# Sigmoid off the last stored gates, gelu at eviction, gates fetched two blocks ahead, combination in another queue

## The chip, the cores and the metric

The kernel runs on one core of one Trainium2 chip. The metric is the device time of one execution in microseconds. A core has a matrix engine (PE, with its weight loads shown as PEld), a vector engine (DVE), a scalar engine for activations (ACT), GpSimd (POOL), and SP, which in this kernel issues nearly all DMAs. Each engine works through its own instructions in the order in which they stand, and waits on semaphores for the others.

## The reference

One layer of a decoder trunk over 1024 prompt positions and 32 sample positions (1056 columns in all), width 1024, all in fp32:

```
h = layer_norm(ALPHA * x + 0.5 * swiglu(x, f1_w1, f1_w3, f1_w2), ln1_g, ln1_b)
z = h @ w_in + b_in                       # q, k, v | u, v of the SGU | gates ga, gb
...
att = combine_groups(outs, lses)          # 3 dilated window groups, softmax weights of the denominators
yb = u * (tril(W_s) LN(v) + b)            # u, v = gelu(uv), chunks of 128
mix = (sigmoid(ga) * (att @ w_oa) + sigmoid(gb) * (yb @ w_ob)) @ w_out
h = layer_norm(ALPHA * h + mix, ln2_g, ln2_b)
h = layer_norm(ALPHA * h + 0.5 * swiglu(h, f2_w1, f2_w3, f2_w2), ln3_g, ln3_b)
```

The prompt's attention has three groups (window, dilation) = (128, 1), (512, 4), (2048, 16) with four heads each. The sample rows attend to stored keys and values.

## The kernel before

Activations lie transposed: 128 channels on the partitions, positions on the free axis, cut into four chunks of 264 columns. A product in fp32 is made of three passes on rounded halves (`mm3`: high x high, high x low, low x high), so one 128 x 264 block over a depth of 1024 is 24 matmuls of 264 columns (`dense8`), and one over a depth of 512 or 256 is 12 or 6. Most large products use a Strassen-like scheme of seven products (`pair`, `hidden`, `seven`).

The program runs `ffn`, `widen`, `mix`, `ffn`. `widen` makes z, 42 blocks of 128 channels by 1056 columns, and stores each in DRAM (`zD`). Blocks 0 to 17 are q, k, v; 18 to 21 are u and 22 to 25 v of the SGU; 26 to 33 and 34 to 41 are the gates ga and gb. Ten of the sixteen gates are made by plain products (`gate8`): the first `NLEAD` = 6 (34 to 39) at the head of `widen`, while the layer norm of the chunks is finishing, and the last `NTAIL` = 4 (30 to 33) in `mix`, where their matmuls fill PE beside the attention. Of the six in `widen`, the first `CHUNKED` come chunk by chunk, all of a chunk's as soon as that chunk is normed; their weights are loaded during the end of `ffn` into tiles of the slot pool. The others come unit by unit. All other blocks come from `pair`, two blocks at a time, which gathers the seven products on ACT and DVE and sends the results to `zD`.

`mix` has two products per output block n of eight: `local(n)` makes gb x (yb @ w_ob), where `mt[n]` is first the gate 34 + n loaded from `zD` and is multiplied by the product at eviction (L1491); the main loop then loads the gate 26 + n into `ta`, multiplies it by att @ w_oa, adds the two (L1552) and splits the sum into halves for `w_out`. `local` of the first four blocks runs ahead of `split_att`, that of the last four inside the loop.

Side work is written as generators in three queues, and `tick` moves them: `bg` (the attention of one head group, `attend`, and `sample_rows`), `slow` (one step per tick: the sample attention, the combination of groups, the joining of the samples) and `mid` (three steps per tick: the SGU). `combine(hp)` is appended when the third group of a half is finished. It fetches the minima and sums of the three groups in twelve small loads from `mlD`, makes the coefficients on DVE, writes them to `cD`, and fetches them back broadcast over the partitions, one group after the other into one buffer `cb`, with a multiply-add for each (L1269 to L1272). `split_att` needs both halves; all products of the main loop need `split_att`. From these generators a scheduler makes each engine's final order.

Tiles of 128 x 1056 come from a pool of 37 slots (`S`); weights pass through two raw buffers (`R`) and eight split ones (`W`). PE's products of `gate8`, `product` and `block` take turns in three PSUM banks (`mm`). On ACT, sigmoid, gelu, exp and square root are in different tables; a table load stands ahead of an activation whose table isn't the present one. Copies and the identity need no load.

## Time and profile before

| | us |
|---|---|
| median of 2 runs | 2310.63 (2310.39 to 2310.87) |
| the profiled execution | 2307.22 |
| its span, first to last instruction | 2305.4 |
| PE busy in it | 2164.4 |
| `mix` up to the first blocks of w_out, about | 1141 to 1498 |
| PE busy in these 357 us | 259.2 |

The profile is of one execution. Its page gives the busy time of each engine and the costliest groups of instructions (a group is a line of the source, an engine, an operation, and what it writes and reads). The trace behind it answers questions by stretch of time: busy time of each engine in it, groups in it, who waited for whom, and the instructions in order of time. In a row of waits stand the waiting line, the one that released it, and total, count and longest. In a row of groups stand the busy time, the mean of one in ns and, behind the bar, the idle time just before them with what ended it. In a row of the timeline stand start, duration, engine, line, operation, and in brackets the idle time before it.

### The profile page before, as it was taken

Reading aid. Unit: us, or ns where it says so; the run is one execution under the profiler, and the core shown is the slowest. Engines: PE = TensorE matmul, PEld = TensorE weight load, DVE = VectorE, ACT = ScalarE, POOL = GpSimd, SP = SyncE. Lnnn points to the kernel's source line nnn. Section 1 sums busy time; section 2 is a strip of 40 time slices with the busy share of each in tenths; the row PEclk is TensorE's granted clock in tenths of the full one; section 3 lists DMA queues with packets and bytes.
Section 4 is the critical chain, followed back from the end, with each engine's and each line's share of the span. In section 5 each row is a group of like instructions: output and inputs, shape, how many; then the busy total and the mean of one; then the engine's idle time right before and its main releaser. Section 6 shows DMA issues by size and latency. Waiting matters only on the chain. (4 is left out here: it accounts for less than half of the span.)

```text
span 2305.4 us, 43046 instructions
## 1 busy us (share of the span) xinstructions
PE 2164.4 (94%) x17209; PEld 2107.5 (91%) x17209; DVE 1576.9 (68%) x2722; ACT 935.5 (41%) x1713; POOL 339.0 (15%) x250
## 2 busy tenths in 40 slices
PE   9999999999998999999898864699999999999997
PEld 8999999999988999999876654699999999999997
DVE  8777767566788337878535465658777777746787
ACT  5444444311136333423388830226444344421124
POOL 0423323000000022232000000000323333200000
PEclk9999999999999999999997886899999999999999
DMA  4445454788753246665744334422355454596731
GB/s 159 140 149 187 154 182 168 262 315 295 296 175 117 80 162 218 204 227 196 265 148 137 105 115 134 174 112 96 129 177 180 159 181 158 186 347 253 274 141 76
DMA packets 161048, 416.83 MB, mean 181 GB/s; under 512 B 23808, under 2 KB 57328, under 8 KB 158160
## 3 DMA queue, kind: packets, MB, share of 16 engines
q1 hardware_dynamic: 160416, 413.55, 51.0%
q8 instruction: 135, 2.21, 0.4%
q14 instruction: 65, 0.53, 0.1%
q10 hardware_dynamic: 432, 0.54, 0.1%
HBM read 301.64 MB, written 158.57 MB: 200 GB/s over the span
## 5 line engine op out<-in xcount | busy, mean ns | idle before, releaser
L224 PE MATMUL ax<-S,W 128*128 128x264 f32 x5688 | 743.0, 284 | 0.6 <-ACT S L975 0.6
L224 PEld LDWEIGHTS ax<-S,W 128*128 128x128 f32 x5688 | 712.7, 188 | 2.3 <-ACT S L975 1.2
L224 PE MATMUL mm<-S,W 128*128 128x264 f32 x4632 | 638.7, 294 | 72.1 <-DVE S L1491 59.1
L224 PEld LDWEIGHTS mm<-S,W 128*128 128x128 f32 x4632 | 605.6, 196 | 84.8 <-DVE S L1491 61.2
L224 PE MATMUL ax<-S,S 128*128 128x264 f32 x3432 | 505.4, 285 | 0.5 <-DVE S L984 0.5
L224 PEld LDWEIGHTS ax<-S,S 128*128 128x128 f32 x3432 | 453.6, 188 | 1.9 <-DVE S L984 0.7
L224 PE MATMUL mm<-S,S 128*128 128x264 f32 x2472 | 390.8, 286 | 14.1 <-ACT S L235 9.5
L224 PEld LDWEIGHTS mm<-S,S 128*128 128x128 f32 x2472 | 337.3, 189 | 16.5 <-ACT S L235 10.0
L235 ACT CAST W<-R 128x1024 fp32r<-128x1024 f32 (+3 forms) x170 | 125.8, 756 | 427.0 <-PE mm L224 195.8
L366 POOL TENSOR_TENSOR Q<-R 128x512 f32<-128x512 f32 x53 | 73.8, 1392 | 847.2 <-DMA R<-w13a 237.4
L235 ACT CAST W<-Q 128x1024 fp32r<-128x1024 f32 (+1 forms) x82 | 80.9, 987 | 233.5 <-POOL Q L367 127.7
L236 DVE TENSOR_TENSOR W<-R,W 128x1024 fp32r<-128x1024 f32 (+3 forms) x170 | 148.1, 878 | 20.7 <-ACT W L235 20.6
L778 DVE SCALAR_TENSOR_TENSOR S<-ax,S 128x264 f32<-128x264 f32 x240 | 98.9, 426 | 58.0 <-PE ax L224 57.4
L441 DVE TENSOR_TENSOR S<-ax,M 128x264 f32<-128x264 f32 x84 | 33.5, 432 | 151.9 <-PE ax L224 151.9
L236 DVE TENSOR_TENSOR S<-Q,S 128x1024 fp32r<-128x1024 f32 (+2 forms) x90 | 127.7, 1419 | 7.1 <-ACT S L235 6.3
L235 ACT CAST S<-Q 128x1024 fp32r<-128x1024 f32 (+2 forms) x90 | 89.5, 994 | 100.6 <-PE ax L224 72.0
L103 POOL CAST S<-ones 128x1 fp32r<-128x1 f32 x32 | 13.5, 444 | 785.5 <-DVE S L1552 382.0
L236 DVE TENSOR_TENSOR W<-Q,W 128x1024 fp32r<-128x1024 f32 (+1 forms) x82 | 94.8, 1156 | 41.1 <-ACT W L235 41.0
L367 POOL TENSOR_TENSOR Q<-Q,R 128x512 f32<-128x512 f32 x53 | 87.6, 1652 | 2.7
L236 DVE TENSOR_TENSOR S<-S,M 128x528 fp32r<-128x528 f32 x72 | 85.3, 1185 | 2.5 <-ACT M L235 0.9
L374 POOL TENSOR_TENSOR Q<-R,Q 128x512 f32<-128x512 f32 x53 | 86.5, 1633 | 1.4
L372 POOL TENSOR_TENSOR Q<-R,R 128x512 f32<-128x512 f32 x53 | 80.7, 1523 | 20.7 <-ACT M L437 13.5
(200 smaller groups left out, 2089.2 us busy)
## 6 DMA issues: line engine op xcount, KB each, us to landing
ws<-st SPq DMA_DIRECT2D x144, 256.0 KB
S<-sumsA SPq DMA_DIRECT2D x63, 528.0 KB
S<-sumsB SPq DMA_DIRECT2D x63, 528.0 KB
M<-kv SPq DMA_DIRECT2D x96, 256.0 KB
sumsA<-M SPq DMA_DIRECT2D x90, 264.0 KB
sumsB<-M SPq DMA_DIRECT2D x90, 264.0 KB
R<-w13b SPq DMA_DIRECT2D x44, 512.0 KB
S<-zD SPq DMA_DIRECT2D x42, 528.0 KB
```

Of the source, the lines that this page charges most:

```text
L103: self.nc.gpsimd.tensor_copy(t[:, 0, :1] if len(shape) == 3 else t[:, :1], self.ones[:, :1])
L224: mm = lambda a, b, s, e: nc.tensor.matmul(o, a[:, cc], b, start=s, stop=e, skip_group_check=True)
L235: a = self.nc.scalar.copy(hi, src)
L236: b = self.nc.vector.tensor_tensor(lo, src, hi.bitcast(F32), op=ALU.subtract)
L366: tt(s12[:, lo], cd[:, lo], cd[:, hi], op=ALU.add)
L367: tt(s12[:, hi], s12[:, lo], ab[:, lo], op=ALU.subtract)
L372: tt(s34[:, lo], ab[:, lo], cd[:, lo], op=ALU.subtract)
L374: tt(s34[:, hi], ab[:, hi], s12[:, hi], op=ALU.subtract)
L441: go(one, 5, False, lambda x: tt(h[:, x, 1], one[x], p7[:, x], op=ALU.add))
L778: nc.vector.scalar_tensor_tensor(y(x, r, e), bank[x], HALF, y(x, r, e), op0=ALU.mult, op1=ALU.add)
```

## The change

Six edits. `CHUNKED` goes from 2 to 3. The four gates made in `mix` are stored without sigmoid; it is applied in the main loop to those blocks, on the loaded tile. The gelu of u and v moves from the SGU's generators into `pair`, in the places where the gates of `pair` already get their sigmoid. Gates are fetched from `zD` two blocks ahead of their use in both `local` and the main loop. `combine` goes into the queue `mid` instead of `slow`, with a buffer for each group's broadcast, and the queues are emptied together by ticks before `split_att`. `sample_rows` pauses four steps, not one, before its transposes.

```diff
-CHUNKED = 2
+CHUNKED = 3
...
-    def gate8(self, w, nb, c, *steps):
+    def gate8(self, w, nb, c, fn, *steps):
...
-            nc.scalar.activation(t, p, AF.Sigmoid, bias=self.bin(nb))
+            nc.scalar.activation(t, p, fn, bias=self.bin(nb))
...
-        gate = n1 >= 26
+        fn = None if n1 < 18 else AF.Gelu if n1 < 26 else AF.Sigmoid
...
-        def sig(t, x, o, n):
+        def bend(t, x, o, n):
             c0 = (2 * x + o) * C
-            nc.scalar.activation(t[:, c0 : c0 + n * C], t[:, c0 : c0 + n * C], AF.Sigmoid)
+            nc.scalar.activation(t[:, c0 : c0 + n * C], t[:, c0 : c0 + n * C], fn)
...
-        go(two, 2, True, add(two, a, 0), *([lambda x: sig(ta, x, 0, 1)] if gate else []))
+        go(two, 2, True, add(two, a, 0), *([lambda x: bend(ta, x, 0, 1)] if fn else []))
...
-        go(three, 4, False, add(three, c, 0), *([lambda x: sig(tc, x, 0, 2)] if gate else []))
+        go(three, 4, False, add(three, c, 0), *([lambda x: bend(tc, x, 0, 2)] if fn else []))
...
-        go(one, 3, False, put(one, a, 1, AF.Sigmoid if gate else AF.Identity))
+        go(one, 3, False, put(one, a, 1, fn or AF.Identity))
...
-            self.slow.append(self.combine(hp))
+            self.mid.append(self.combine(hp))
...
-        cb = self.S([P, NP])
-        for g in range(3):
+        cbs = [self.S([P, NP]) for _ in range(3)]
+        for g, cb in enumerate(cbs):
             for h in range(2):
                 nc.sync.dma_start(cb[64 * h : 64 * h + 64], self.cD[hp, g, h].partition_broadcast(64))
-            yield
-            yield
+        yield from self.pause(3)
+        for g, cb in enumerate(cbs):
             aT = self.attT.pop((hp, g))
...
     def sample_rows(self, *blocks):
...
-        yield
+        yield from self.pause(4)
...
-        for t in self.vr:
-            nc.scalar.activation(t, t, AF.Gelu)
-            yield
...
-        nc.scalar.activation(u, u, AF.Gelu)
-        yield from self.pause(1)
...
         def local(n):
             wb = self.unit(a["wo"][n, :, 2 * P :], 4 * P)
-            mt[n] = self.fetch_z(34 + n)
+            if n + 2 < KB:
+                mt[n + 2] = self.fetch_z(36 + n)
...
-                self.gate8(units[n], DENSE[NLEAD + n], c, STEPS["tail"], 1)
+                self.gate8(units[n], DENSE[NLEAD + n], c, AF.Identity, STEPS["tail"], 1)
         units = self.A = None
+        for n in range(2):
+            mt[n] = self.fetch_z(34 + n)
...
-        self.drain()
+        ta = [self.fetch_z(26 + n) for n in range(2)]
+        while self.bg or self.mid or self.slow:
+            self.tick(1, 1)
         split_att()
...
-            wa, ta = self.unit(a["wo"][n], 2 * P), self.fetch_z(26 + n)
+            wa = self.unit(a["wo"][n], 2 * P)
+            if n + 2 < KB:
+                ta.append(self.fetch_z(28 + n))
             if n < KB // 2:
                 local(KB // 2 + n)
+            if 26 + n in DENSE:
+                nc.scalar.activation(ta[n], ta[n], AF.Sigmoid)
             for c in range(NC):
-                product(wa, att, c, ta)
+                product(wa, att, c, ta[n])
                 self.tick(2)
-            nc.vector.tensor_tensor(mt[n], mt[n], ta, op=ALU.add)
+            nc.vector.tensor_tensor(mt[n], mt[n], ta[n], op=ALU.add)
```

The calls of `gate8` in `widen` pass `AF.Sigmoid`. The change adds lines, so the lines of the new program are counted from the new file; those quoted in the rows below are of their own program.

ACT's order where the first head group's softmax meets the tail gates, in the kernel before. L935 is `gate8`'s activation, L1157 the exp of the softmax, L1332 the sample attention's exp, L1172 a copy of transposed probabilities:

```order
L1157 ACTIVATE S_13462,X_13460<-S_13462,X_13460 128x256
L935 ACT_TABLE_LOAD
L935 ACTIVATE M_13610<-mm_13585,cols 128x264
L1332 ACT_TABLE_LOAD
L1332 ACTIVATE X_12833,X_12836<-X_12833,X_12836 128x132
L935 ACT_TABLE_LOAD
L935 ACTIVATE M_13723<-mm_13698,cols 128x264
L1172 COPY S_13529<-ax_13521 128x2x128
L1172 COPY S_13529<-ax_13522 128x512
L935 ACTIVATE M_13777<-mm_13752,cols 128x264
L1157 ACT_TABLE_LOAD
L1157 ACTIVATE S_13532,X_13460<-S_13532,X_13460 128x256 x4
```

The same place in the changed kernel, with the same lines:

```order
L1157 ACTIVATE S_13478,X_13476<-S_13478,X_13476 128x256
L935 ACTIVATE M_13626<-mm_13601,cols 128x264
L1332 ACTIVATE X_12849,X_12852<-X_12849,X_12852 128x132
L935 ACTIVATE M_13739<-mm_13714,cols 128x264
L1172 COPY S_13545<-ax_13537 128x2x128
L1172 COPY S_13545<-ax_13538 128x512
L935 ACTIVATE M_13816<-mm_13791,cols 128x264
L1157 ACTIVATE S_13548,X_13476<-S_13548,X_13476 128x256 x4
```

The order of the work is the same; the four table loads of this place are gone. In the whole program there are 49 table loads before and 19 after.

SP's order from the second half's combination into the main loop, before. L1257 stores the coefficients, L1264 fetches them broadcast (two loads per group), L1083 fetches a gate from `zD`, L214 loads a weight, L1523 rows of w_out for column sums, L207 copies state:

```order
L1257 DMA cD<-S_15483 16x128 x3
L1264 DMA S_15516<-cD 64x1024 x6
L1083 DMA S_15573<-zD 128x1056
L1083 DMA S_15582<-zD 128x1056
L1523 DMA Q_15672<-wout 128x1024
L214 DMA R_15921<-wo 128x256
L207 DMA ws<-st 16x4096
L1523 DMA Q_15734<-wout 128x1024
L214 DMA R_15930<-wo 128x512
L207 DMA ws<-st 16x4096
L1083 DMA S_15694<-zD 128x1056
```

The same stretch in the changed kernel, with the same lines:

```order
L1257 DMA cD<-S_15439 16x128 x3
L1264 DMA S_15472<-cD 64x1024 x2
L1264 DMA S_15473<-cD 64x1024 x2
L1264 DMA S_15474<-cD 64x1024 x2
L1083 DMA S_15488<-zD 128x1056
L1083 DMA S_15551<-zD 128x1056
L1083 DMA S_15553<-zD 128x1056
L1083 DMA S_15593<-zD 128x1056
L1083 DMA S_15602<-zD 128x1056
L1523 DMA Q_15754<-wout 128x1024
L214 DMA R_15948<-wo 128x512
```

The six broadcast loads go into three buffers instead of one, and five gate loads stand behind them where two stood.

PE's order at the end of the last head group, before. L1168 turns probabilities, L1206 the minima and sums of the group, L1184 multiplies by v, L224 are the output products:

```order
L1168 MATMUL ax_15348<-ident,S_15305 128x128
L1168 MATMUL ax_15349<-ident,S_15305 128x128
L1206 MATMUL ax_15393<-ident,X_15142 32x128
L1184 MATMUL ax_15343<-S_15354,Q_15102 64x128 x4
L224 MATMUL mm_15398<-S_14525,W_15321 128x264
L224 MATMUL mm_15398<-S_14526,W_15321 128x264
L224 MATMUL mm_15398<-S_14525,W_15322 128x264
```

The same place in the changed kernel; L1376 is the transpose of the joined sample rows:

```order
L1168 MATMUL ax_15371<-ident,S_15328 128x128
L1168 MATMUL ax_15372<-ident,S_15328 128x128
L1206 MATMUL ax_15413<-ident,X_15201 32x128
L1376 MATMUL ax_15568<-ident,X_15563 128x128
L1184 MATMUL ax_15366<-S_15377,Q_15161 64x128 x4
L224 MATMUL mm_15650<-S_14426,W_15596 128x264
L224 MATMUL mm_15650<-S_14427,W_15596 128x264
```

Behind the last L1184 there follow, before, nine blocks of twelve matmuls that do not need the combined attention, with L1376 between the eighth and the ninth; in the changed kernel one such block follows, and the other eight stand earlier, among the steps of the last head group.

More of the change, by code (lines that the diff above doesn't have):

```diff
@@ L1055, in widen @@
             for n in range(CHUNKED):
-                self.gate8(units[n], DENSE[n], c, STEPS["lead"], 1)
+                self.gate8(units[n], DENSE[n], c, AF.Sigmoid, STEPS["lead"], 1)
         units = Y = None
@@ L1062, in widen @@
             for c in (1, 3, 0, 2):
-                self.gate8(w, DENSE[n], c, STEPS["lead"], 1)
+                self.gate8(w, DENSE[n], c, AF.Sigmoid, STEPS["lead"], 1)
                 if n == NLEAD - 1:
```

## Prediction

> **What bounds the kernel now.** I read the page's busy shares first, then the busy time by stretches for the stage between the last input-projection pairs and the output projection.
>
> ```profile
> PE 2164.4 (94%) x17209; PEld 2107.5 (91%) x17209; DVE 1576.9 (68%) x2722; ACT 935.5 (41%) x1713; POOL 339.0 (15%) x250
> core 0: us, PE busy (x) PEld busy (x) DVE busy (x) ACT busy (x) POOL busy (x), PEclk, DMA share, GB/s
> 750.00:775.00 25.00, 25.00 (x208) 25.00 (x208) 11.28 (x10) 11.85 (x18) 2.70 (x3) 1.00 0.37 116
> 875.00:900.00 25.00, 25.00 (x208) 24.97 (x207) 22.36 (x35) 8.08 (x17) 8.20 (x6) 1.00 0.70 234
> 1157.00:1330.00 173.00, 147.47 (x1021) 112.08 (x1020) 75.92 (x277) 146.23 (x316) 0.00 (x0) 0.86 0.37 124
> 1352.00:1401.00 49.00, 15.20 (x105) 14.41 (x103) 25.55 (x54) 5.45 (x10) 0.00 (x0) 0.68 0.47 139
> 1401.00:1498.00 97.00, 66.63 (x421) 64.70 (x422) 60.98 (x92) 17.42 (x21) 3.65 (x10) 0.79 0.46 159
> 1141.00:1498.00 357.00, 259.22 (x1762) 216.57 (x1761) 183.20 (x499) 184.99 (x395) 3.65 (x10) 0.82 0.43 143
> ```
>
> Over the span PE is the bound: in a stretch of dense work it is busy without a gap, 208 matmuls in 25 us, so 0.120 us for one of 264 columns. The 357 us of `mix` are different. Weight loads, which follow each other without modelled tails, fill 216.6 us, so at least 140 us of that stage is not PE's own work. It has three parts with different limits: the attention (1157 to 1330), where ACT is busy 146 of 173 us; the 49 us after it, where PE is nearly empty; and the loop over eight output blocks (97 us), where no engine is full. The waits of PE, asked by stretch (680 to 760; 760 to 1141; 1141 to 1358, three rows; 1401 to 1500), name what ends last:
>
> ```profile
> PE mm L224 <- ACT S L235: 5.5, 2, 4.8
> PE ax L1280 <- ACT S L975: 5.4, 4, 2.6
> PE ax L1168 <- ACT S L1157: 18.8, 8, 6.7
> PE ax L1184 <- ACT S L1172: 3.2, 6, 0.9
> PE mm L224 <- ACT M L935: 2.6, 1, 2.6
> PE mm L224 <- DVE S L1491: 53.6, 8, 24.4
> ```
>
> **Term 1, activation tables and gelu in the attention stage.** The groups of ACT between 1141 and 1352 us:
>
> ```profile
> L1157 ACT ACT_TABLE_LOAD x16 | 20.5, 1283 | 0.3
> L935 ACT ACT_TABLE_LOAD x13 | 16.7, 1283 | 1.5 <-issue 1.3
> L1449 ACT ACT_TABLE_LOAD x4 | 5.1, 1283 | 0.1
> L1408 ACT ACTIVATE S<-S 128x1056 f32<-128x1056 f32 x4 | 4.4, 1092 | 0.0
> L1449 ACT ACTIVATE S<-S 128x1056 f32<-128x1056 f32 x4 | 4.3, 1084 | 0.0
> L1408 ACT ACT_TABLE_LOAD x2 | 2.6, 1283 | 0.0
> L1332 ACT ACT_TABLE_LOAD x1 | 1.3, 1283 | 0.0
> L624 ACT ACT_TABLE_LOAD x1 | 1.3, 1283 | 0.0
> ```
>
> The 16 tail gates apply sigmoid, the softmax applies exp, the SGU gelu, and ACT's order alternates them: 37 loads of 1.283 us, 47.5 us. With identity at the gates and no gelu here, the new order holds 3 loads in this stage (exp, sqrt, exp). That is 34 x 1.283 = 43.6 us less, and the eight gelus (4.4 + 4.3 = 8.7 us) go too: 52.3 us of ACT. How much of it is on the path? Upper end: all, 52, if ACT alone sets the pace (it is 85% busy, and PE's weight loads leave 173 - 112 = 61 us, so PE does not take it back sooner). Lower end: the visible waits of PE for ACT, 18.8 + 3.2 + 2.6 = 24.6. I take 40, nearer to the busy share, because a load sits directly between a score and its exp, the step that PE's transposes wait for. PE's order also puts eight more 12-matmul blocks of the output work ahead of the last attention step: 8 x 12 x 0.120 = 11.5 us. Most of it fills holes; I charge 4 here, up to 10 at the lower end. Net **36**, from 15 to 52.
>
> Whether more than 1.283 us is lost per switch is seen in the timeline of ACT:
>
> ```profile
> 1156.70 0.48 ACT L935 ACTIVATE M<-mm,cols 128x264 f32<-128x264 f32 x1 [5.37 <-DMA zD<-M]
> 1157.20 1.28 ACT L1157 ACT_TABLE_LOAD   x1
> 1158.50 0.40 ACT L1157 ACTIVATE S<-S,X 128x128 f32<-128x128 f32 x1
> ```
>
> The load starts 0.02 us after the gate's activation ends and the exp 0.02 us after the load. [...]
>
> The gelus do not vanish: they are done on the pairs' results, where ACT is busy 8 to 12 of 25 us and PE never waits for it (rows 750 and 875). Four pairs get some 2.2 us of ACT each plus three further loads: **0**, because ACT's idle half hides it and the added step works on SBUF after the PSUM bank was read. If that cover were gone, 8.7 + 3.8 = 12.5 us.
>
> **Term 2, the combination after the last head group.** Timelines of PE and DVE there:
>
> ```profile
> 1343.37 0.39 DVE L1244 TENSOR_TENSOR X<-X,S 16x128 f32<-16x128 f32 x1
> 1348.62 0.87 DVE L1255 TENSOR_TENSOR S<-X,S 16x128 f32<-16x128 f32 x3
> 1351.60 0.27 PE L1206 MATMUL ax<-ident,X 128*32 128x128 f32 x1
> 1357.63 1.11 DVE L1491 TENSOR_TENSOR S<-S,mm 128x264 f32<-128x264 f32 x3 [7.30 <-DMA S<-zD]
> 1359.79 0.27 DVE L1208 COPY X<-ax 32x128 f32<-32x128 f32 x1
> 1377.83 0.86 DVE L1255 TENSOR_TENSOR S<-X,S 16x128 f32<-16x128 f32 x3
> 1384.13 1.23 DVE L1269 TENSOR_TENSOR S<-S,S 128x1024 f32<-128x1024 f32 x1 [5.01 <-DMA S<-cD]
> 1389.97 1.23 DVE L1271 TENSOR_TENSOR S<-S,S 128x1024 f32<-128x1024 f32 x1 [3.38 <-DMA S<-cD]
> 1395.77 1.23 DVE L1271 TENSOR_TENSOR S<-S,S 128x1024 f32<-128x1024 f32 x1 [3.32 <-DMA S<-cD]
> 1401.10 10.73 PE L224 MATMUL mm<-S,W 128*128 128x264 f32 x72 [24.39 <-DVE S L1491]
> ```
>
> From the last attention transpose (1351.6) to the first product that needs the result (1401.1) it takes 49.5 us. Inside it: 8.2 us until the small copy of L1208, which stood in DVE's queue behind a gate load; 18.9 us until the coefficients are done at 1378.7, although the same arithmetic for the first half took 6.1 us (1343.4 to 1349.5), the rest being loads behind the other half's combination on SP; 5.4 us to the first broadcast; then three broadcasts 5.8 us apart, because one buffer serves them all; then 5.3 us. After: copy 1, its round trip and the twelve small loads 8, arithmetic 6, first broadcast 5.4, the other two close behind from their own buffers 4, last multiply-add and split 5.3: 29.7 (2 and 4 are my estimates from the 5.8 us that a broadcast now takes with its wait). The saving is 49.5 - 30 = **19**. Upper end 27, with loads and broadcasts at half of what I gave them; lower end 5, only the stand behind the gate load. What is late next is this same chain, now with a single block of PE work beside it instead of nine.
>
> **Term 3, gates two blocks ahead.** The evictions of the loop, from the groups between 1401 and 1498 us:
>
> ```profile
> L1491 DVE TENSOR_TENSOR S<-S,mm 128x264 f32<-128x264 f32 x48 | 18.9, 425 | 27.8 <-DMA S<-zD 16.9 <-PE mm L224 10.8
> ```
>
> DVE waits 16.9 us for gate loads, and as long as it does, PE's three banks stay full and PE waits (53.6 - 24.4 = 29 us of L224 after L1491 in the loop). DVE's own work is 61 of 97 us, so it would be the next bound. Gain: 16.9 plus half of the 10.8 that DVE loses to a PE that is catching up, **22**; upper end 34 (97 down to DVE's 61 and 2 us of seams), lower end 10, if the loads, now bunched behind the broadcasts on SP, land late for half of the blocks. The four sigmoids added to the loop, 4 x 1.09 and one load, 5.7 us, lie on an ACT that is busy 17 of 97 us, ahead of use: 0, and 4.4 if a load arrives only then.
>
> **Terms 4 and 5, lead by chunk and sample rows.** A third gate per chunk gives PE 24 x 0.120 = 2.9 us more work for each of three chunks before the last chunk is needed, against 5.5 us of waits for ACT's casts: **5**, from 0 (third weight unit late for want of a slot) to 5.5. The transposes of L1280 wait 5.4 us for an eviction; pausing four steps instead of one moves them behind it: **4**, from 0 to 5.4.
>
> **Sum.** 36 + 19 + 22 + 5 + 4 = 86 us off a profiled span of 2305.4 us, 2219. That execution took 2307.2 us, the median shown is 2310.6, so on its scale 2310.6 - 86 = **2225**. All upper ends give 124, so 2187; all lower ends 30, so 2281.
>
> **The rivals.** *ACT was not the pace.* The transposes of one head group follow each other like this:
>
> ```profile
> 1270.75 0.44 PE L1168 MATMUL ax<-ident,S 128*128 128x128 f32 x2 [2.78 <-ACT S L1157]
> 1274.74 0.66 PE L1168 MATMUL ax<-ident,S 128*128 128x128 f32 x4
> 1278.02 0.66 PE L1168 MATMUL ax<-ident,S 128*128 128x128 f32 x4
> ```
>
> A step from score to transpose and back takes 3.3 to 4 us, through PE, DVE, ACT and PE again. If that chain sets the pace, only 15 remain in term 1: 65 in all, so 2246. Against it: ACT's 85%. 0.13. *Loads late again.* SP has a queue in order and slots are short with three broadcast buffers and two gates ahead; terms 2 and 3 give 8 each: 61, so 2250. 0.12; both together 40, so 2271, 0.10. *Slower.* The combination of the first half now stands in the fast queue: if its twelve loads and stores hold SP while weights wait behind them, its chain, up to the 49.5 us of the second half's, lies bare too, terms 2 and 3 vanish, and terms 1, 4 and 5 leave 36 + 9 - 49.5 = -4.5; with term 1 at its lower end it is 25 us slower, 2336. It decides from the point where that stand is longer than the 45 us which terms 1, 4 and 5 give; the longest stand behind a load that the rows above show is 7.3 us. 0.06. [...] 0.04. That the loads would not go is excluded by ACT's new order, 19 loads in all against 49.
>
> **Numbers.** Forecast 0.55 at 2225. To hold 8 in 10 the range goes from 2189 to 2274, which takes in the first two rivals and most of both together. Two per cent, about what a measurement of this kernel can tell from no change, is 46 us, 2264. Faster: the forecast, both single rivals, the costlier switch and a share of both together, 0.84; within 0.11; slower 0.05.
>
> **What would show it.** In the new profile: ACT's table loads at L1157 and L935 down to 2 or 3 in the attention and ACT below 75% busy there; the stretch from the first tail gate to the last L1206 some 175 us, not 211; about 30 us from that L1206 to the first product of the loop, with the three broadcast multiplies under 3 us apart; DVE's wait for zD in the loop near 0 and the loop at about 75 us; no wait at the sample transposes. It is wrong if the attention stage shrinks by under 20 us, or if SP stands behind a load that waits for a slot.

## The result and the profile after

The changed kernel takes 2232.84 us, median of 2 runs (2231.18 to 2234.50), against 2310.63: a ratio of 0.9667, 95% interval 0.9644 to 0.9691, so 77.8 us or 3.3% less. The forecast was 2225, the range 2189 to 2274. The total is where it was expected; the parts of it are not. In one experiment below (both halves slow, three outputs' blocks later) one of four executions took 4358.90 us; it counts in the median shown there, not in the ratio.

The profiled execution took 2234.5 us with a span of 2232.6 us. To compare kernels I cut the span at four marks that all of them have: the first transpose of the attention (L1125), the last transpose of its row sums (L1206), the start of the last multiply-add of the combination (L1272), and the first eviction of a w_out block. The stretches between them are called start, attention, tail, loop and rest.

| us, from one profiled execution each | start | attention | tail | loop | rest |
|---|---|---|---|---|---|
| before | 1148.7 | 202.9 | 45.4 | 100.3 | 808.0 |
| after | 1135.1 | 196.0 | 24.3 | 67.1 | 810.2 |
| difference | -13.7 | -6.9 | -21.1 | -33.2 | +2.2 |

Three quarters of the gain lie in the loop and the tail, and the attention, for which the largest term was forecast, gave 7 us. On the page of the profile PE is now busy nearly throughout, and by stretches (attention, tail up to the first product, loop) DVE is the busiest engine of the loop: 60 of 68 us.

```profile
PE 2143.9 (96%) x17209; PEld 2091.9 (94%) x17209; DVE 1574.3 (71%) x2722; ACT 899.4 (40%) x1695; POOL 344.7 (15%) x250
...
core 0: us, PE busy (x) PEld busy (x) DVE busy (x) ACT busy (x) POOL busy (x), PEclk, DMA share, GB/s
1135.00:1331.00 196.00, 176.37 (x1318) 143.66 (x1319) 104.60 (x371) 110.38 (x322) 0.00 (x0) 0.91 0.48 156
1331.00:1354.00 23.00, 3.83 (x28) 2.81 (x25) 13.54 (x29) 3.91 (x8) 0.00 (x0) 0.67 0.66 193
1354.00:1422.00 68.00, 56.63 (x405) 53.87 (x405) 60.18 (x91) 23.27 (x26) 7.88 (x10) 0.91 0.58 200
```

In the attention (1120 to 1340) ACT's table loads are down to three, as the order said, and ACT is busy 110 of 196 us:

```profile
L1157 ACT ACT_TABLE_LOAD x2 | 2.6, 1283 | 0.0
L624 ACT ACT_TABLE_LOAD x1 | 1.3, 1283 | 0.0
```

The waits of PE in the pairs (760 to 1135), in the attention (1127 to 1335) and in the loop (1354.5 to 1422) show what is left. The wait at the sample transposes is gone, with 3.6 us of a new one behind it; the wait for the exps fell from 18.8 to 14.4 us only; the loop's wait for evictions fell from 29 to 8.9 us:

```profile
PE ax L224 <- DVE S L984: 3.6, 6, 1.1
...
PE ax L1168 <- ACT S L1157: 14.4, 5, 5.9
...
PE mm L224 <- DVE S L1486: 8.9, 8, 3.2
```

DVE's product evictions in the loop (now L1486) wait for no gate any more; before, 16.9 us of their 27.8 us of idle time ended on a load from `zD`:

```profile
L1486 DVE TENSOR_TENSOR S<-S,mm 128x264 f32<-128x264 f32 x44 | 17.8, 425 | 3.3 <-PE mm L224 3.2
```

The waits are not all of it. Cut at the marks, the loop before and after:

```profile
1397.03:1497.32 100.29, 66.43 (x420) 64.50 (x420) 63.48 (x94) 18.46 (x22) 3.65 (x10) 0.78 0.45 155
1355.36:1422.42 67.06, 55.41 (x402) 52.65 (x400) 58.85 (x88) 23.27 (x26) 7.88 (x10) 0.92 0.57 197
```

Of the 33.2 us, 22.2 are idle time of PE that went (33.9 to 11.7 us), and 11.0 are PE's own busy time, which fell with 18 matmuls fewer and a granted clock of 0.92 instead of 0.78.

The tail, in the timelines of DVE and PE: the small copy L1208 follows its transpose at once, and the three broadcast multiplies stand 2.3 and 2.2 us apart instead of 5.8. From L1206 at 1331.06 to the first product that needs the result it takes 23.1 us, before 49.5, forecast 30.

```profile
1331.37 0.28 DVE L1208 COPY X<-ax 32x128 f32<-32x128 f32 x1 [1.95 <-PE ax L1206]
...
1340.65 0.87 DVE L1255 TENSOR_TENSOR S<-X,S 16x128 f32<-16x128 f32 x3
1347.25 1.23 DVE L1269 TENSOR_TENSOR S<-S,S 128x1024 f32<-128x1024 f32 x1 [5.73 <-DMA S<-cD]
...
1349.54 1.23 DVE L1271 TENSOR_TENSOR S<-S,S 128x1024 f32<-128x1024 f32 x1 [0.76 <-DMA S<-cD]
1351.72 1.23 DVE L1271 TENSOR_TENSOR S<-S,S 128x1024 f32<-128x1024 f32 x1 [0.96 <-DMA S<-cD]
...
1354.14 1.69 PE L224 MATMUL mm<-S,W 128*128 128x264 f32 x6 [14.13 <-DVE S L236]
```

Where the attention's gain went shows when it is cut at the six L1206, one for each head group: 33.7, 35.5, 27.4, 31.6, 23.0 and 44.8 us, before 37.2, 42.0, 29.2, 31.6, 34.7 and 28.2. Five groups became 23.4 us shorter, the last one 16.6 us longer. The timelines of PE and DVE in that last group:

```profile
1290.36 0.71 PE L1145 MATMUL ax<-S,S 64*128 64x128 f32 x4
...
1295.81 13.42 PE L224 MATMUL mm<-S,W 128*128 128x264 f32 x108
1311.72 0.48 PE L1168 MATMUL ax<-ident,S 128*128 128x128 f32 x1 [2.49 <-ACT S L1157]
...
1296.14 0.40 DVE L1244 TENSOR_TENSOR X<-X,S 16x128 f32<-16x128 f32 x1
...
1302.75 0.89 DVE L1255 TENSOR_TENSOR S<-X,S 16x128 f32<-16x128 f32 x3
...
1309.71 1.23 DVE L1269 TENSOR_TENSOR S<-S,S 128x1024 f32<-128x1024 f32 x1 [3.99 <-DMA S<-cD]
1310.85 0.28 DVE L1153 CUSTOM_DVE_ANT_0 S<-ax,M 128x128 f32<-128x128 f32 x1
```

The first scores are in PSUM at 1291, and DVE takes them up 20 us later (L1153): in its order the combination of the first half up to its first broadcast multiply stands ahead, with the wait for the broadcast. Meanwhile PE works off 108 matmuls of other blocks in one piece. Whether those blocks or DVE's order make the group long was the first question for the experiments.

### The profile page after: what moved, and what is told of

Read it like the earlier page. It is cut to its first block, busy times and chain, and to the rows that moved or that the text cites. A ratio compares the mean times of both kernels' runs of the same rounds, so it can differ in the third digit from the quotient of the medians.

```text
span 2232.6 us, 43026 instructions
## 1 busy us (share of the span) xinstructions
PE 2143.9 (96%) x17209; PEld 2091.9 (94%) x17209; DVE 1574.3 (71%) x2722; ACT 899.4 (40%) x1695; POOL 344.7 (15%) x250
## 4 chain that ended last, share of the span: by engine, by line
PE 84%; DVE 6%; DMA 5%; ACT 2%; issue 1%; POOL 1%; SPq 1%; ACTq 0%; DVEq 0%; POOLq 0%
PE ax L224 46%; PE mm L224 34%; DMA M<-kv 1%; PE ax L1145 1%; DVE S L236 1%; PE ax L1168 1%; DVE W L236 1%; PE ax L1184 1%; DMA S<-cD 1%; DMA S<-zD 1%; DMA R<-wz 1%; DMA S<-hD 0%; DVE S L602 0%; DVE S L1486 0%; ACT S L235 0%
## 5 line engine op out<-in xcount | busy, mean ns | idle before, releaser
L224 PE MATMUL ax<-S,W 128*128 128x264 f32 x5688 | 744.3, 285 | 0.5 <-ACT S L975 0.3
L224 PEld LDWEIGHTS ax<-S,W 128*128 128x128 f32 x5688 | 712.4, 188 | 3.0 <-ACT S L975 1.4
L224 PE MATMUL mm<-S,W 128*128 128x264 f32 x4536 | 616.1, 291 | 41.5 <-DVE S L236 15.2
L224 PEld LDWEIGHTS mm<-S,W 128*128 128x128 f32 x4536 | 582.2, 193 | 55.7 <-DVE S L236 17.6
L224 PE MATMUL ax<-S,S 128*128 128x264 f32 x3432 | 507.3, 285 | 3.9 <-DVE S L984 3.6
L224 PEld LDWEIGHTS ax<-S,S 128*128 128x128 f32 x3432 | 453.8, 188 | 6.8 <-DVE S L984 5.7
L224 PE MATMUL mm<-S,S 128*128 128x264 f32 x2568 | 403.1, 286 | 7.8 <-ACT S L235 4.2
L224 PEld LDWEIGHTS mm<-S,S 128*128 128x128 f32 x2568 | 349.7, 189 | 9.8 <-ACT S L235 4.4
L235 ACT CAST W<-R 128x256 fp32r<-128x256 f32 (+2 forms) x169 | 124.8, 755 | 375.2 <-PE mm L224 144.5
L236 DVE TENSOR_TENSOR W<-R,W 128x256 fp32r<-128x256 f32 (+2 forms) x169 | 146.9, 876 | 25.0 <-ACT W L235 24.9
L235 ACT CAST W<-Q 128x1024 fp32r<-128x1024 f32 (+1 forms) x82 | 80.9, 987 | 203.1 <-POOL Q L367 95.8
L236 DVE TENSOR_TENSOR S<-Q,S 128x1024 fp32r<-128x1024 f32 (+2 forms) x90 | 125.9, 1399 | 6.0 <-ACT S L235 5.4
L103 POOL CAST S<-ones 128x1 fp32r<-128x1 f32 x32 | 19.3, 628 | 715.4 <-DVE S L236 558.7
L235 ACT CAST S<-Q 128x1024 fp32r<-128x1024 f32 (+2 forms) x90 | 89.4, 994 | 99.4 <-PE ax L224 71.7
L236 DVE TENSOR_TENSOR W<-Q,W 128x1024 fp32r<-128x1024 f32 (+1 forms) x82 | 94.9, 1157 | 32.8 <-ACT W L235 32.8
L236 DVE TENSOR_TENSOR S<-S,M 128x528 fp32r<-128x528 f32 x72 | 84.7, 1177 | 2.8 <-ACT M L235 0.9
L235 ACT CAST S<-R 128x512 fp32r<-128x512 f32 (+1 forms) x68 | 46.2, 683 | 96.7 <-DMA sumsA<-S 42.2
```

What stands on the lines that cost most here:

```text
L103: self.nc.gpsimd.tensor_copy(t[:, 0, :1] if len(shape) == 3 else t[:, :1], self.ones[:, :1])
L224: mm = lambda a, b, s, e: nc.tensor.matmul(o, a[:, cc], b, start=s, stop=e, skip_group_check=True)
L235: a = self.nc.scalar.copy(hi, src)
L236: b = self.nc.vector.tensor_tensor(lo, src, hi.bitcast(F32), op=ALU.subtract)
```

## The experiments

Times are medians. Since the batches' times of the kernel before differ by some us (2311.7 to 2313.7), kernels are compared by their ratios to it; one thousandth is 2.3 us. The changed kernel stands at 0.9667. The stretches between the marks come from one profiled execution each, which lies up to 7 us off the median of its kernel. The start alone, with the same program in it, ends between 1130.9 and 1139.8 us in the changed kernel and in nine of the experiments.

**The table edits alone.** The kernel before, with the last gates' sigmoid in the loop and gelu at eviction:

```diff
-            nc.scalar.activation(t, p, AF.Sigmoid, bias=self.bin(nb))
+            nc.scalar.activation(t, p, fn, bias=self.bin(nb))
...
-        gate = n1 >= 26
+        fn = None if n1 < 18 else AF.Gelu if n1 < 26 else AF.Sigmoid
...
+            if 26 + n in DENSE:
+                nc.scalar.activation(ta, ta, AF.Sigmoid)
```

> The kernel before with two of the six edits alone: the last four gates stored without sigmoid (applied in the main loop) and gelu at the pairs' eviction. No other edit, and PE's order keeps the eight blocks of the output work behind the last attention step. Theory (ACT was the pace of the attention): the stretch from the first L1125 to the last L1206 falls from 202.9 us by some 25 us, what the first five head groups lost in the changed kernel (23.4 us), and the tail and the loop stay at 49.5 and 97 us: 2310.6 - 25 = 2286, between 2280 and 2292. The recorded term, 40 us without the charge for the moved blocks, would give 2271. Rival (the chain through four engines was the pace, ACT was only busy): under 10 us, 2301 to 2310.

Measured: 2294.45 us, ratio 0.9924 (0.9899 to 0.9949), 17.6 us less. The attention took 178.7 us, 24.2 less, as the theory said; the tail is unchanged (45.5). The total missed the expected 2280 to 2292, since the loop did not stay: it grew from 100.3 to 108.2 us. With gates still loaded at use, the sigmoid (L1545 here) stands between the load and the eviction, and DVE waited 10.1 us for it:

```profile
L1486 DVE TENSOR_TENSOR S<-S,mm 128x264 f32<-128x264 f32 x48 | 19.0, 425 | 34.5 <-DMA S<-zD 14.2 <-ACT S L1545 10.1 <-PE mm L224 10.1
```

So the two parts of the change need each other: the late sigmoid is free only where the gates come early. The windows of the attention, of this kernel and of the one before:

```profile
1150.20:1328.90 178.70, 161.83 (x1223) 129.29 (x1223) 93.63 (x347) 108.69 (x320) 0.00 (x0) 0.92 0.44 148
```

```profile
1148.50:1351.60 203.10, 175.50 (x1222) 136.03 (x1223) 93.76 (x347) 160.99 (x362) 0.00 (x0) 0.87 0.38 129
```

52.3 us fewer on ACT made the stage 24.2 us shorter. PE is then busy 162 of 179 us. Its waits for ACT in the attention, 18.8 + 3.2 + 2.6 = 24.6 us before, are now 13.5:

```profile
PE ax L1168 <- ACT S L1157: 9.7, 2, 5.9
PE mm L224 <- ACT M L935: 2.7, 2, 2.0
PE ax L1184 <- ACT S L1172: 1.1, 4, 0.4
```

So the waits account for some 11 us, and the other 13.7 are PE's busy time, which fell from 175.5 to 161.8 us for the same number of matmuls.

**The table edits undone.** The changed kernel with sigmoid back in `gate8`, gelu back in the SGU's generators and no sigmoid in the loop.

```diff
-        fn = None if n1 < 18 else AF.Gelu if n1 < 26 else AF.Sigmoid
+        fn = AF.Sigmoid if n1 >= 26 else None
...
+        for t in self.vr:
+            nc.scalar.activation(t, t, AF.Gelu)
+            yield
...
+        nc.scalar.activation(u, u, AF.Gelu)
+        yield from self.pause(1)
```

The sigmoid's part of the edit is shown with the next kernel.

> The changed kernel with these two edits undone and the other four kept: 49 table loads instead of 19, PE's order as in the changed kernel, with 205 matmuls of the output work and the last gates in the last head group. Theory: some 25 us slower than the changed kernel, 2258, between 2250 and 2268, all of it ahead of the last L1206. Rival (chain): under 10 us, 2233 to 2243. If the loads hide where PE now has a long stretch of its own work in the last group, the price falls there and not in the first five groups.

Measured: 2261.47 us, ratio 0.9786 (0.9758 to 0.9813), 27 us over the changed kernel; attention 227.2 us, 31.2 more, tail and loop as in the changed kernel (24.6 and 66.5). The theory holds in its size and its place; most is in the first, second and fifth group (40.2, 40.5 and 35.9 us). Again half of the 31.2 us is PE's busy time, 192.1 us against 176.4 in the changed kernel.

**Sigmoid alone back.**

```diff
-                self.gate8(units[n], DENSE[NLEAD + n], c, AF.Identity, STEPS["tail"], 1)
+                self.gate8(units[n], DENSE[NLEAD + n], c, AF.Sigmoid, STEPS["tail"], 1)
...
-            if 26 + n in DENSE:
-                nc.scalar.activation(ta[n], ta[n], AF.Sigmoid)
```

> The changed kernel with sigmoid back at the last four gates and no sigmoid in the loop; the gelus stay at the pairs' eviction. 40 table loads instead of 19: 21 x 1.283 = 27 us of ACT in the attention, 5.7 us less of it in the loop. Theory (half to two thirds of ACT's time lies on the path): 13 to 18 us slower than the changed kernel, 2248 to 2253. Rival (the gelus of the SGU were the dear part: in the kernel before, the fifth head group held three of them and shrank by 12 of the 24 us): under 10 us, 2238 to 2244.

Measured: 2249.65 us, ratio 0.9730 (0.9702 to 0.9759), 15 us over; attention 211.9, 15.9 more. 22 more loads in it, 28 us, cost 16; the gelus and their loads are the other half of the 31.

**More switches.**

```diff
+            nc.scalar.activation(self.X([P, 2], "warm", 1), self.ones[:, :2], AF.Sigmoid)
             for h in range(2):
                 for r in range(2):
                     i = 2 * t + r
```

> The changed kernel with a sigmoid of two columns put ahead of the exps of each attention step, 24 in all: 45 table loads instead of 19, so 26 more, and 24 short activations, nothing else. ACT gets 26 x 1.283 = 33.4 us and some 5 us for the activations. By the price found for the tables in the attention stage (24 to 31 us for 47 to 52 us of ACT, a half to two thirds): 19 to 26 us slower than the changed kernel, 2253 to 2261. [...] Rival (PE alone sets the pace since the tables went): under 8 us, 2233 to 2242.

Measured: 2260.12 us, ratio 0.9771 (0.9740 to 0.9802), 24 us over, within the theory's 19 to 26. The attention took 226.0 us, 30 more, in a profiled execution 6 us above the median. ACT's timeline shows no time lost beside the loads of 1.283 us: in the attention every load begins at most 0.02 us after the activation ahead of it, and the next activation at most 0.02 us after the load.

```profile
1155.48 0.48 ACT L935 ACTIVATE M<-mm,cols 128x264 f32<-128x264 f32 x1 [1.17 <-DMA zD<-M]
1155.97 1.28 ACT L1148 ACT_TABLE_LOAD   x1
1157.27 0.20 ACT L1148 ACTIVATE X<-ones 128x2 f32<-128x2 f32 x1
1157.49 1.28 ACT L1158 ACT_TABLE_LOAD   x1
1158.79 0.51 ACT L1158 ACTIVATE S<-S,X 128x256 f32<-128x256 f32 x1
```

**Gates loaded at use again.**

```diff
-            if n + 2 < KB:
-                mt[n + 2] = self.fetch_z(36 + n)
+            mt[n] = self.fetch_z(34 + n)
...
-            if n + 2 < KB:
-                ta.append(self.fetch_z(28 + n))
+            ta.append(self.fetch_z(26 + n))
```

> The changed kernel with the gates loaded in the block that uses them, as before; all else kept. The order then leaves eight of the twelve-matmul blocks behind the last attention step, as the kernel before does. Theory: the loop loses the 28 us that it gained, and the last head group gains back about 14 us that the moved blocks cost it, since they stand there in one stretch of 108 matmuls in 13.4 us with no attention in it: net 10 to 16 us slower, 2243 to 2249. Rival (the moved blocks only filled holes): 28 us slower, 2258 to 2263. Rival (the loop's gain came from elsewhere): no slower than 2236.

Measured: 2271.65 us, ratio 0.9829 (0.9805 to 0.9853), 37 us over: more than the theory and both rivals expected. The loop took 97.3 us, 30 more, near the 28 expected. The last head group stayed at 44.2 us although the eight blocks stood behind it. That does not clear the blocks: here PE's products that were left in the group stood 14.91 us behind DVE's order and were worked off among the scores. The tail grew by 7, since three evictions wait for a gate ahead of the combination's multiplies on DVE. In its timelines the coefficients are ready at 1344, and the first multiply starts at 1356.4:

```profile
1314.00 5.65 PE L224 MATMUL mm<-S,W 128*128 128x264 f32 x24 [14.91 <-DVE S L1486]
...
1343.16 0.87 DVE L1255 TENSOR_TENSOR S<-X,S 16x128 f32<-16x128 f32 x3
1355.35 1.11 DVE L1486 TENSOR_TENSOR S<-S,mm 128x264 f32<-128x264 f32 x3 [11.32 <-DMA S<-zD]
1356.38 1.22 DVE L1269 TENSOR_TENSOR S<-S,S 128x1024 f32<-128x1024 f32 x1
```

**Four outputs' blocks written after the attention.**

```diff
-        for n in range(KB // 2):
+        for n in range(0):
+            local(n)
+        while self.bg:
+            self.tick(1, 1)
+        for n in range(0, 4):
             local(n)
```

> The changed kernel with one thing more: the first four output blocks of yb @ w_ob are written after the last attention step and not before it, so that nine blocks of twelve matmuls (instead of one) stand between the last L1206 and the first product of the loop; gates still two blocks ahead. Theory: the last head group shrinks from 44.8 us to about 30 and the tail stays at 23 to 26 us, since PE works 4 of its 23 us: 11 to 14 us faster than the changed kernel, 2219 to 2222. Rival (the blocks filled holes beside the attention): 2230 to 2236. Rival (their evictions delay the combination on DVE, as a block's did by 7.3 us before): tail over 30 us and 2228 to 2240.

Measured: 2233.58 us, ratio 0.9658 (0.9632 to 0.9683): no difference from the changed kernel that can be told. The last group fell to 35.7 us, though DVE took up its first scores 18 us after they were made, the tail rose to 26.3 and the loop to 78.3. DVE's order has the blocks' evictions behind the multiplies, so with its three PSUM banks full PE stood 22.8 us, and the blocks came back in the loop:

```profile
1344.51 32.55 PE L224 MATMUL mm<-S,W 128*128 128x264 f32 x240 [22.79 <-DVE S L1486]
```

**The combination as before.**

```diff
-            self.mid.append(self.combine(hp))
+            self.slow.append(self.combine(hp))
...
-        cbs = [self.S([P, NP]) for _ in range(3)]
-        for g, cb in enumerate(cbs):
+        cb = self.S([P, NP])
+        for g in range(3):
...
-        yield from self.pause(3)
-        for g, cb in enumerate(cbs):
+            yield
+            yield
...
-        while self.bg or self.mid or self.slow:
-            self.tick(1, 1)
+        self.drain()
```

> The changed kernel with the combination as before: both halves in the slow queue, one broadcast buffer, the queues emptied as before. Theory (the first half's combination in the fast queue costs the last head group what the tail gains): DVE's order has the scores of the last group ahead of the first broadcast multiply again, so the group falls from 44.8 us to 30 to 35 (PE has 163 matmuls of other work in it, 19.6 us, beside some 12 of its own), and the tail goes back from 23 to 45 to 49 us: net 8 to 16 us slower than the changed kernel, 2241 to 2249. Rival (the recorded term: the edit only shortens the tail, the last group is long because of the moved blocks): group stays at 44 us, net 22 to 26 us slower, 2255 to 2259.

Measured: 2237.10 us, ratio 0.9672 (0.9655 to 0.9689), the same as the changed kernel within the intervals; both expectations were too high. The group is as the theory had it: 32.7 us, 12.1 less. The tail took 37.9 us, 13.6 more, and not 45 to 49. So this edit, worth 19 in the forecast, gains 14 us in the tail and loses 12 in the attention.

**The first half alone back in the slow queue.**

```diff
-            self.mid.append(self.combine(hp))
+            (self.mid if hp else self.slow).append(self.combine(hp))
```

> The changed kernel with only the first half's combination back in the slow queue (the second half's stays in the fast one; three buffers in both). DVE's order then has the last group's scores ahead of the broadcast multiplies. Theory (stall on DVE behind the first combination): the last group falls from 44.8 us to about 35, where PE's 186 matmuls (22.3 us) and the group's own 12 us fill it; the tail stays at 23 to 27 us: 6 to 10 us faster than the changed kernel, 2223 to 2227. Rival (the last group is long because PE has 201 matmuls in it, the stall is hidden under them): group 42 to 45 us, 2231 to 2236.

Measured: 2232.29 us, ratio 0.9657 (0.9641 to 0.9674), not told apart from the changed kernel in total. In the trace the last group is 35.8 us, as the theory had it, and PE works in it without a gap, so now the moved blocks do set its length; the tail took 28.8 us. The expected 6 to 10 us do not show in the ratio.

```profile
1283.90:1319.80 35.90, 35.87 (x283) 31.45 (x280) 24.38 (x87) 16.23 (x53) 0.00 (x0) 1.00 0.45 122
```

**Both halves slow, three outputs' blocks later.** As the last one for both halves, with `local(0)` alone ahead of the end of the attention.

```diff
-            self.mid.append(self.combine(hp))
+            self.slow.append(self.combine(hp))
...
-        for n in range(KB // 2):
+        for n in range(1):
+            local(n)
+        while self.bg:
+            self.tick(1, 1)
+        for n in range(1, 4):
             local(n)
```

> The changed kernel with both combinations in the slow queue, each with three buffers, and the output blocks of n = 1 to 3 written after the last attention step. PE has 153 matmuls of other work in the last group and five blocks of twelve behind it, and DVE's order has three evictions between the small arithmetic and the first broadcast multiply of the second half. Theory: last group 30 to 33 us, tail 23 to 26 us with four or five blocks hidden in it: 11 to 15 us faster than the changed kernel, 2218 to 2222. Rival (blocks in the tail are held behind the multiplies on DVE and come back in the loop): the loop 5 us longer and 2225 to 2230.

Measured: 2229.63 us, ratio 0.9642 (0.9624 to 0.9660), 6 us under the changed kernel with the intervals overlapping, so the expected 11 to 15 us are not shown. The last group was 37.5 us, not 30 to 33: the arithmetic of the first half now stands ahead of the first scores and among them. Tail 26.2, loop 67.4: no blocks came back.

**The lead by chunk and the sample rows' pause undone.**

```diff
-CHUNKED = 3
+CHUNKED = 2
...
-        yield from self.pause(4)
+        yield
```

> The changed kernel with the lead by chunk at two gates and one pause ahead of the sample transposes, as before. Recorded terms: 5 + 4 = 9 us slower, 2242, read apart in the trace: PE's waits between 680 and 760 us at 7 us instead of 0.4, and the waits of the sample transposes at 5 us instead of 0. Rival (a later stage takes it up, since PE then arrives earlier at the stage that waits for stored blocks): under 4 us, 2233 to 2237.

Measured: 2249.53 us, ratio 0.9728 (0.9712 to 0.9744), 14 us over, good to 7; the attention starts 11.8 us later (1146.85). The waits of PE (600 to 760, and 760 to 1150) are back: those for ACT's casts (L235) and at the sample transposes (L1280) have no row in the changed kernel's answers, those for DVE are 3.3 and 0.4 us there:

```profile
PE mm L224 <- DVE S L866: 4.8, 3, 3.1
PE mm L224 <- ACT S L235: 4.1, 2, 3.5
PE mm L224 <- DVE S L236: 1.4, 2, 0.9
...
PE ax L1280 <- ACT S L975: 6.0, 4, 2.2
```

**The order mended.** Both combinations slow, a pause ahead of the arithmetic, and the first four outputs' blocks after the attention (a second kernel has 18 in place of 12):

```diff
-            self.mid.append(self.combine(hp))
+            self.slow.append(self.combine(hp))
...
-        yield
+        yield from self.pause(3 if hp else 12)
...
+        while self.bg:
+            self.tick(1, 1)
         for n in range(KB // 2):
             local(n)
```

> The changed kernel with the order around the combination mended: both combinations in the slow queue, a pause of 12 ticks (3 for the second half) between the small loads and the arithmetic, and the first four output blocks written after the last attention step. On DVE the first broadcast multiply then stands behind all scores of the last group, and behind the last attention step evictions of nine blocks stand among the combination's steps, four of them between the second half's arithmetic and its first broadcast multiply, where DVE has waited 5.7 us for the broadcast. Theory (DVE's order sets both): last group 28 to 31 us instead of 44.8, tail 24 to 28 us, loop 68 to 70 us: 8 to 14 us faster than the changed kernel, 2219 to 2227, a ratio to before of 0.960 to 0.9635. Rival (the work of PE is only moved about, and comes back in the loop): 2228 to 2235, ratio over 0.964.

> As the one before with a pause of 18 ticks: nine evictions stand ahead of the second half's arithmetic, five of them inside it, none in the wait for the broadcast. Theory (order on DVE): last group as there, but the second half's chain carries the blocks' time, 1.44 us a block: tail 28 to 32 us, 3 to 5 us slower than with 12. Rival: no difference, since PE's blocks run at the same pace in both.

Measured with 12 ticks: 2214.40 us, ratio 0.9579 (0.9553 to 0.9606), below both kernels and 20 us under the changed one, the intervals apart; 8 to 14 were expected. Attention 172.9 us (last group 26.5; the fourth and fifth are 6 us shorter too), tail 27.4, loop 67.6.

With 18 ticks: 2228.91 us, ratio 0.9635 (0.9610 to 0.9659); last group 26.5 as well, but a tail of 39.0 us, 12 longer rather than 3 to 5. The expectation overlooked the first half: after the longer pause its own broadcasts land only in the tail, and DVE waits for them there:

```profile
1311.17 1.23 DVE L1269 TENSOR_TENSOR S<-S,S 128x1024 f32<-128x1024 f32 x1 [3.71 <-DMA S<-cD]
```

In the timelines of DVE and PE with 12 ticks, the last group's scores no longer wait for a broadcast, 96 matmuls of other blocks run in the tail, and three of their evictions lie between the coefficients and the multiply, whose wait for the broadcast is 2.25 us instead of 5.73:

```profile
1292.57 0.27 DVE L1153 CUSTOM_DVE_ANT_0 S<-ax,M 128x128 f32<-128x128 f32 x1
...
1308.71 0.28 DVE L1208 COPY X<-ax 32x128 f32<-32x128 f32 x1 [2.43 <-PE ax L1206]
1308.92 1.20 DVE L1269 TENSOR_TENSOR S<-S,S 128x1024 f32<-128x1024 f32 x1
...
1321.04 0.89 DVE L1255 TENSOR_TENSOR S<-X,S 16x128 f32<-16x128 f32 x3
1321.86 0.96 DVE L1486 TENSOR_TENSOR S<-S,mm 128x264 f32<-128x264 f32 x2
1323.83 0.43 DVE L1486 TENSOR_TENSOR S<-S,mm 128x264 f32<-128x264 f32 x1 [1.01 <-PE mm L224]
...
1327.57 1.22 DVE L1269 TENSOR_TENSOR S<-S,S 128x1024 f32<-128x1024 f32 x1 [2.25 <-DMA S<-cD]
...
1314.05 14.15 PE L224 MATMUL mm<-S,W 128*128 128x264 f32 x96 [4.33 <-DVE S L1486]
```

Four of these kernels answer what made the last head group long. All have the tables moved and the gates early; they differ in where the output blocks stand, and in whether the first half's broadcast multiply stands ahead of the group's first scores on DVE. The second half's combination begins only behind this group.

| last head group, us (its matmuls of other work) | blocks behind the last attention step | blocks ahead of it |
|---|---|---|
| multiply behind the scores | 26.5 (105), 12 ticks | 35.8 (186), first half slow |
| multiply ahead of the scores | 35.7 (105), four outputs' blocks after | 44.8 (201), the changed kernel |

Each of the two, the blocks ahead and the multiply ahead, costs about 9 us, with the other or without it.

## Why the prediction was right in its sum and wrong in its parts

| | recorded, us | undone in the changed kernel, us | by the marks |
|---|---|---|---|
| term 1, tables and gelu, with the blocks' charge | 36 (15 to 52) | 27 | attention 31; done alone 24 |
| term 2, combination | 19 (5 to 27) | 1 | tail 14 gained, last group 12 lost |
| term 3, gates two ahead | 22 (10 to 34) | 37 | loop 30, tail 7 |
| terms 4 and 5 | 9 (0 to 10.9) | 14 | start 11.8 |
| sum | 86 | 79 | 73 between the spans |

Each number of the third column is a difference of two ratios with intervals of some 2.5 thousandths, so it is good to 7 or 8 us; the parts depend on each other, so that they add up to the whole is not given. The blocks move with the gates, so they are undone in the third row, not in the first. The sum came out because two terms were too large by 27 us together and two too small by 20: the 2225 was hit by cancelling errors, which is luck, not by four right sizes. By its own sign, an attention stage that shrinks by under 20 us, the prediction was wrong where it put its largest term: the attention shrank by 6.9. The tables gave 24 there, and the blocks and the first half's multiply took 9 each.

**Term 1.** The mechanism is right (loads between a score and its exp cost time, and they went), the size was 40 where 24 is shown alone and 27 to 31 undone. The step that failed is the choice of 40, "nearer to the busy share", with its support that PE's weight loads leave 61 us. PE's own busy time left 27.6 us of 203.1 before and leaves 16.9 of 178.7 once the tables are gone. ACT's 85% was true and still half hidden. That the 24.6 us of visible waits come so near to the 24.2 is luck: only 11 us of them went, and 13.7 came from PE's busy time, of which the prediction says nothing.

Beside it, "I charge 4" for the eight blocks put ahead of the last attention step was too little. "Most of it fills holes" is what failed: they cost 9 us, close to the 10 of the lower end, and PE is busy in 35.87 of the group's 35.90 us where they are alone. The 81 matmuls more are worth 81 x 0.120 = 9.7 us.

**Term 2.** The tail's steps were as forecast, even 7 us shorter: from the end of the small copy to the coefficients it takes 9.9 us where 8 + 6 was put. (The recorded 6.1 us for the first half's arithmetic begins at its third operation; from L1242 at 1339.11 it is 10.4.) The failed step is that the change was priced at the second half alone. The recorded slower rival had the mechanism, the first half's combination lying bare in the fast queue, but looked for it on SP; it stands on DVE, ahead of the last group's scores, and took 9 us. The undone edit shows 12, but its group also has 38 fewer matmuls of other work (163 and 201). And the part of term 2 that removes the "stand behind the gate load" of the small copy belongs to term 3: with the combination as before and gates early the tail is 37.9 us, not 45.4.

**Term 3.** Right mechanism, under-sized: undone it is worth 30 us in the loop and 7 in the tail, where evictions that wait for a gate hold up the combination. The term counted idle time of DVE alone, 16.9 and half of 10.8. In the loop PE's waits behind L1491 fell from 29 to 8.9 us, and PE's own busy time fell by 11 us beside them. The loop, 67 us, is near the bound that was named, DVE's 61.

**Terms 4 and 5.** Not told apart from the recorded 9: 14 is good to 7 us, and the 11.8 of the start to some 4. In the traces with these edits undone and done, PE's waits differ by 4.1 for the casts and 6.0 at the transposes, near the recorded sizes, and by 2.5 more for DVE in the lead (L866 and L236: 6.2 against 3.7), with 1.1 us of a new wait behind the transposes: 11.5 us in all.

Of the tells, ACT's share (56%), three table loads, the 23 us tail, the broadcasts 2.2 us apart, no wait for `zD` and a loop of 68 us came true or were better (30 us and 75 us had been named for the tail and the loop). The stretch from the first tail gate (1129.08) to the last L1206 did not: 202 us, forecast 175. That tell, and the sign of being wrong, pointed at the fault. The costlier switch that the chances name is shown by no run: with the added switches, gaps of at most 0.02 us stand around loads of 1.283 us in ACT's timeline. That ACT was not the pace at all is excluded by the four kernels with table loads moved or added, in which 29 to 52 us of ACT were worth 16 to 31 us of the stage.

## What to carry to other kernels

Do not size the relief of an engine by its busy share: 52 us off ACT were worth 24 here. Look at what the engine next in line has left to do in its own row, and at its waits; and where the granted clock is lower with more idle time, as here (0.87 with 27.6 us of it in the attention before, 0.92 with 16.9 once the tables are moved), count on its busy time to fall too (about as much again in these four kernels). When a queue is made faster, price every piece of work in it: a short chain with a round trip through DRAM that is brought forward stands on its engine ahead of whoever comes next, here 9 us. Work that "fills holes" has to be held against the holes of that very stretch: the eight blocks cost 9 us. Work meant to fill a hole needs its evictions in the hole too; here moving blocks alone changed nothing in the total, and moving them with the multiplies' order gave 20 us.

## What the runs showed of the hardware

The same number of matmuls did not keep PE busy for the same time. The attention of the kernel before and that with the tables moved hold 1222 and 1223 matmuls, and PE was busy 175.5 and 161.8 us, at a granted clock of 0.87 and 0.92; where PE hardly waited (the last group with the first combination slow, busy 35.87 of 35.90 us) the clock was 1.00, and in the tail of the changed kernel, with PE busy 3.8 of 23 us, 0.67. So of the 24.2 us some 13.7 were PE working faster and 10.5 were idle time that went. Busy time times granted clock stayed nearly the same: 152.7 and 148.9 us there, and with 1318 or 1319 matmuls 160.5 in the changed kernel (176.4 at 0.91), 160.3 with sigmoid alone back (184.3 at 0.87), 160.8 with more switches (193.7 at 0.83) and 165.2 with the tables back (192.1 at 0.86). By an estimate from these rows the clock alone makes 175.5 x 0.87 / 0.92 = 166.0, so 9.5 of the 13.7. What sets the granted clock no run here isolates.

With more switches a table switch between queued activations cost its load and no more: 24 two-column sigmoids took 0.20 us each, with gaps of at most 0.02 us around 1.283 us loads.
